# LayerNorm shift rows added by accumulating DMAs, gMLP's v normalised on ScalarE, and gates summed along the free dimension

## The chip, the cores and the metric

The kernel runs on one core of one Trainium2 chip. The metric is device time in microseconds (us), the median of several runs. A profile is one execution of the same program. In its rows PE is TensorE's matmuls, PEld its weight loads, DVE VectorE, ACT ScalarE, POOL GpSimd, and SP SyncE, which here issues DMA.

## The reference, cut to what matters

Two layers (l = 0, 1) with three sub-layers each work on x of 256 rows by 1024 columns. Each sub-layer scales and shifts its input by numbers computed from a vector c, runs a block, multiplies the block's output by a gate that is also computed from c, and normalises:

```
c_act = silu(c)
mod   = c_act @ w_ada[l] + b_ada[l]              # nine rows of 1024 for each layer
shift, scl, gate = mod[3i], mod[3i+1], 1 + mod[3i+2]
h = x * (1 + scl[i]) + shift[i]
x = layer_norm(ALPHA * x + w * gate[i] * block(h), ln_g[l, i], ln_b[l, i])
layer_norm(x, g, b) = (x - mean) * rsqrt(var + 1e-5) * g + b
```

Block 0 and block 2 are SwiGLU feed-forwards (w = 0.5, inner width 2816). Block 1 is the gMLP in layer 0 and chunked attention in layer 1 (w = 1). In the gMLP, z = gelu(h @ w_in + b_in) is split into u and v (2048 columns each); v gets a layer_norm of its own with rows v_g and v_b, then for each of 8 groups of 256 columns a 128x128 matrix mixes its rows, and the result is multiplied into u and by w_out.

## The kernel before, in words

The 256 rows are two tiles t = 0, 1 of 128 rows; X[t] is the residual, 128x1024 in SBUF. Weights stream through once: SP loads a tile `raw` of 128x1024 fp32 (512 KB, six buffers), ACT casts it to `hi` (L215), DVE makes the rest `lo` = raw - hi (L216), and PE does three matmuls of 128x512 for each half of the tile: hi with the high part of the activations (L259), lo with the high part (L260), hi with the low part (L262).

The 20 rows of modulation are computed in between ("steps", one 512 KB tile of w_ada each, pumped between weight units). Fourteen of them (those in the list COLS) are columns: a tile has the 128 features on the partitions and the 1024 elements of c along the free dimension, and DVE multiplies by a row of c and sums along the free dimension in one instruction (L125), which is followed by a read of its accumulator; the result is a tile `mod` of 128x8. The other six are the gates (l, 2), (l, 5), (l, 8), which are needed as rows, repeated on all partitions: DVE adds c[p] * raw into a 128x1024 accumulator `acc` (L154, eight tiles for each gate; POOL clears it, L150, and the bias row is loaded into it, L151). Five ticks of the work list later (LAG_M) `finish_gate` splits acc into ghi (ACT, L166) and glo (DVE, L167), and PE sums over the partitions by matmuls with a matrix of ones (L172, L173, four for each gate); ACT writes the row `gate` from PSUM (L174). `add_y` (L350) multiplies a block's output by it.

After a sub-layer `normalise` computes mean and variance on DVE; POOL takes the power -0.5 (L368), for the gMLP's v as for X; DVE normalises X (L374). `residual_affine` then multiplies X by the row lng (L393) and adds the row lnb (L394), in halves of 512 columns, some 20 ticks later. The rows are loaded, repeated on all partitions, by `load_lnrow`; only at the last of the six LayerNorms is the affine part done elsewhere.

In the gMLP, `v_norm` (one call for each t, four tiles V of 128x512) does (v - mu) * v_g (L581) and * rs + v_b (L582) on DVE, out of rows v_g and v_b that SP has loaded.

`after(n, f)` puts f off by n ticks of the work list; each engine then works its own queue in order.

Of the kernel before, what the change touches and what calls it, by code (L numbers as in the profile page):

```python
# [8 lines left out]
F32 = mybir.dt.float32  # L9
F32R = mybir.dt.float32r  # L10
AF = mybir.ActivationFunctionType
ALU = mybir.AluOpType
AX = mybir.AxisListType

P = 128
D = 1024
SEQ = 256
NT = SEQ // P
KD = D // P
# [19 lines left out]
LAG_A = 4  # L39
LAG_H = (4, 4)  # L40
LAG_H2 = 2
LAG_M = 5

LAG_R = (20, 16)

# [1 line left out]

COLS = [(0, 1), (0, 0), (0, 4), (0, 3), (0, 7), (0, 6), (1, 1), (1, 0), ("kv", 1), ("kv", 0),
        (1, 4), (1, 3), (1, 7), (1, 6)]


@with_exitstack
def encoder_kernel(ctx, tc, a, out):
    nc = tc.nc
    PSUM = bass.MemoryType.PSUM
    pool = lambda name, bufs, **kw: ctx.enter_context(tc.tile_pool(name=name, bufs=bufs, **kw))

    const = pool("const", 1)
    rawp = pool("rawp", N_RAW)
    unitp = pool("unitp", N_UNIT)  # L60
    htp = pool("htp", 8)
    bigp = pool("bigp", N_BIG)
    xp = pool("xp", 1)
    rowp = pool("rowp", 1)
    accp = pool("accp", 1)
    sgp = pool("sgp", 5)
    ap_ = pool("ap", 4)
    bcp = pool("bcp", 2)
    smp = pool("smp", 4)
    modp = pool("modp", 6)  # L70
    ps = pool("ps", 6, space=PSUM)
    pt = pool("pt", 2, space=PSUM)
# [3 lines left out]
    def nm(s):  # L76
        uid[0] += 1
        return f"{s}_{uid[0]}"
# [5 lines left out]
    X = [xp.tile([P, D], F32, name=f"X{t}") for t in range(NT)]  # L84
    c_act = const.tile([P, KD], F32, name="c_act")
    bcol = const.tile([P, len(COLS), KD], F32, name="bcol")
    ident = const.tile([P, P], F32, name="ident")
    make_identity(nc, ident)
    nc.scalar.activation(c_act, c_raw, AF.Silu)
    ones = const.tile([P, P], F32, name="ones")  # L90
    nc.vector.memset(ones, 1.0)
    ones_r = const.tile([P, P], F32R, name="ones_r")
    nc.vector.tensor_copy(ones_r, ones)
    mhalf = const.tile([P, 1], F32, name="mhalf")
    nc.vector.memset(mhalf, -0.5)
    wcol = {}
    for w in (0.5, 1.0):
        wcol[w] = const.tile([P, 1], F32, name=f"wcol{int(2 * w)}")
        nc.vector.memset(wcol[w], w)
    lncols = const.tile([P, 2, 6, KD], F32, name="lncols")  # L100
    bs_sb = const.tile([P, NG], F32, name="bs_sb")
    wsT = const.tile([P, NG, P], F32, name="wsT")
# [1 line left out]
    def load_first():  # L104

        nc.sync.dma_start(out=bcol, in_=a["b_cols"])
        nc.vector.tensor_scalar(bcol[:, 0::2], bcol[:, 0::2], 1.0, None, op0=ALU.add)

    def load_small():
        for t in range(NT):  # L110
# [18 lines left out]
    def col_slice(key):  # L129
        ci = COLS.index(key)  # L130
        st = {}

        def step(j):
            if j == 0:
                st["m"] = modp.tile([P, KD], F32, tag="mod", name=nm("mod"))
            column(ci, j, st["m"])
            if j == KD - 1:
                mods[key] = st["m"]
        return [lambda j=j: step(j) for j in range(KD)]

    def gate_slice(key):
        w_src = a["w_gate"][key[0] * 3 + key[1] // 3].rearrange("(p j) n -> p j n", j=KD)
        b_src = a["b_gate"][key[0] * 3 + key[1] // 3][None, :]
        finish = finish_gate(key, 1.0 if key[1] == 5 else 0.5)
        st = {}

        def step(j):
            if j == 0:
                st["acc"] = accp.tile([P, D], F32, tag="acc", name=nm("acc"))
                nc.gpsimd.memset(st["acc"], 0.0)  # L150
                nc.sync.dma_start(out=st["acc"][0:1, :], in_=b_src)  # L151
            raw = rawp.tile([P, D], F32, tag="raw", name=nm("raw"))
            nc.sync.dma_start(out=raw, in_=w_src[:, j, :])
            nc.vector.scalar_tensor_tensor(st["acc"], raw, c_act[:, j:j + 1], st["acc"],  # L154
                                           op0=ALU.mult, op1=ALU.add)
            if j == KD - 1:
                after(LAG_M, lambda: finish(st["acc"]))
        return [lambda j=j: step(j) for j in range(KD)]

    mods = {}  # L160

    def finish_gate(key, w):
        def f(acc):
            hi = unitp.tile([P, D], F32R, tag="hi", name=nm("ghi"))
            lo = unitp.tile([P, D], F32R, tag="lo", name=nm("glo"))
            nc.scalar.copy(hi, acc)  # L166
            nc.vector.tensor_tensor(lo, acc, hi.bitcast(F32), op=ALU.subtract)  # L167
            g = rowp.tile([P, D], F32, tag="gate", name=nm("gate"))
            for n in range(2):
                sl = slice(n * 512, (n + 1) * 512)  # L170
                tp = pt.tile([P, 512], F32, tag="pt", name=nm("gps"))
                nc.tensor.matmul(tp, lhsT=ones_r, rhs=hi[:, sl], start=True, stop=False)  # L172
                nc.tensor.matmul(tp, lhsT=ones_r, rhs=lo[:, sl], start=False, stop=True)  # L173
                nc.scalar.activation(g[:, sl], tp, AF.Identity, bias=wcol[w], scale=w)  # L174
            mods[key] = g
        return f

    def mk_slice(key):
        return col_slice(key) if key in COLS else gate_slice(key)

    ada = {"steps": [], "credit": 0.0}

    def ada_phase(*parts):

        for _, s in ada["steps"]:
            s()
        ada["steps"] = [(units / (KD * len(keys)), s) for keys, units in parts
                        for k in keys for s in mk_slice(k)]
        ada["credit"] = 0.0

    def pump():
# [9 lines left out]
    def small_dma(out_, in_):  # L201

        with tc.issue_after(last["dma"].ins):
            nc.sync.dma_start(out=out_, in_=in_)
# [62 lines left out]
    def after(n, fn):  # L267
        late.append([n, fn])
# [91 lines left out]
    def rstd_of(parts):  # L360
        stats = smp.tile([P, len(parts), 6], F32, tag=f"st{len(parts)}", name=nm("st"))
        for i, x_ in enumerate(parts):
            nc.vector.bn_stats(out=stats[:, i, :], in_=x_)  # L363
        mv = smp.tile([P, 2], F32, tag="mv", name=nm("mv"))
        nc.vector.bn_aggr(out=mv, in_=stats)
        rs = smp.tile([P, 2], F32, tag="rs", name=nm("rs"))
        nc.vector.tensor_scalar(rs[:, 0:1], mv[:, 1:2], EPS, None, op0=ALU.add)
        nc.gpsimd.tensor_tensor(rs[:, 1:2], rs[:, 0:1], mhalf, op=ALU.pow)  # L368
        return mv[:, 0:1], rs[:, 1:2]
# [6 lines left out]
    lnrow = {}  # L376

    def load_lnrow(ln):
        g = rowp.tile([P, D], F32, tag="lng", name=nm("lng"))
        b = rowp.tile([P, D], F32, tag="lnb", name=nm("lnb"))  # L380
        small_dma(g, a["ln_g"][ln:ln + 1, :].partition_broadcast(P))
        small_dma(b, a["ln_b"][ln:ln + 1, :].partition_broadcast(P))
        lnrow[ln] = (g, b)

    waiting = [[], []]

    def residual_affine(t, ln):

        g, b = lnrow[ln]

        def part(sl):
            with tc.issue_after(last["lo"].ins):
                nc.vector.tensor_tensor(X[t][:, sl], X[t][:, sl], g[:, sl], op=ALU.mult)  # L393
                nc.vector.tensor_tensor(X[t][:, sl], X[t][:, sl], b[:, sl], op=ALU.add)  # L394
            waiting[t].remove(sl)
        waiting[t] = [slice(i * 512, (i + 1) * 512) for i in range(2)]
        for i in range(2):
            after(LAG_R[t] + 2 * i, lambda sl=waiting[t][i]: part(sl))
# [163 lines left out]
    def gmlp(gate, done, before_last):  # L562
# [11 lines left out]
        vrow = []  # L574

        def v_norm(t):
            mu, rs = rstd_of(V[t])
            for n in range(4):
                v = V[t][n]
                g, b = vrow[n]  # L580
                nc.vector.scalar_tensor_tensor(v, v, mu, g, op0=ALU.subtract, op1=ALU.mult)  # L581
                nc.vector.scalar_tensor_tensor(v, v, rs, b, op0=ALU.mult, op1=ALU.add)  # L582

        for vi in range(2):
            c0 = GH + vi * D
            units = row_units(w_in, 0, KD, c0)
            bts = bias_tiles(c0)
            if vi == 1:
                for n in range(4):
                    sl = slice(n * 512, (n + 1) * 512)  # L590
                    gb = []
                    for src in ("v_g", "v_b"):
                        x_ = bigp.tile([P, 512], F32, tag="b", name=nm(src))
                        small_dma(x_, a[src][:, sl].partition_broadcast(P))
                        gb.append(x_)
                    vrow.append(gb)
            for t in range(NT):
                accs = gemm_pass(Later(hT, t), units, KD)
                for n in range(2):
                    v = V[t][vi * 2 + n]  # L600
                    nc.vector.tensor_tensor(v, accs[n], bts[n], op=ALU.add)
                    nc.scalar.activation(v, v, AF.Gelu)
                if vi == 1:
                    v_norm(t)
# [186 lines left out]
    def step(ln):  # L791
# [5 lines left out]
        start=lambda: (ada_phase(([(0, 2)], 13), ([(0, 4), (0, 3)], 24)),))  # L797
# [68 lines left out]
```

## Time and profile before

| | us |
|---|---|
| median of 3 runs | 1056.77 (1054.62 to 1057.21) |
| the profiled execution's own time | 1057.11 |
| span of the profiled execution | 1055.3 |
| PE busy | 1028.1 (97%) |
| PEld busy | 842.2 (80%) |
| DVE busy | 856.0 (81%) |
| ACT busy | 519.9 (49%) |
| POOL busy | 24.5 (2%) |
| data queue of the DMA engines | 76.6% of 16 engines' span, 267 GB/s |

The span is what the profile's rows cover; the execution's own time is 1.8 us more. Busy shares are means over the whole span. In a row of the timeline the first number is the start and the second how long the instructions lasted, from the first's start to the last's end; back-to-back instructions overlap, so what one costs its engine is read from start to start.

### The profile page before, as it was taken

The numbers are of one execution on the slowest core, as the hardware profiler recorded it, in microseconds if no ns is written. First come the engines' busy times: TensorE is split into PE (matmuls) and PEld (weight loads), VectorE is DVE, ScalarE is ACT, GpSimd is POOL, SyncE is SP. The second block draws the span as 40 slices with busy tenths as digits, with TensorE's granted clock in tenths as the row PEclk, the third lists the DMA queues.
The fourth block names the chain that finished last, engine by engine and source line by source line (L and its number), as shares of the span: only waits on it lengthen the run. The fifth ranks groups of instructions, "written<-read, shape, count | busy, mean of one in ns | idle before, by whom it ended". The sixth has DMA issues, their size and how long they took to land. (4 is left out here: it accounts for less than half of the span.)

```text
span 1055.3 us, 13549 instructions
## 1 busy us (share of the span) xinstructions
PE 1028.1 (97%) x4804; PEld 842.2 (80%) x4804; DVE 856.0 (81%) x1185; ACT 519.9 (49%) x729; POOL 24.5 (2%) x39
## 2 busy tenths in 40 slices
PE   7999999999999999999999999999999999999997
PEld 6768888887778788888877888887787788888886
DVE  6888897799999899998679986858998969555535
ACT  4455455454436464444547444453658557345520
POOL 0000000001000100000000000000000000000000
PEclk9999999999999999999999999999999999999999
DMA  9989898687799779999847897757799837645621
GB/s 332 375 315 354 282 348 340 209 280 258 264 333 324 252 251 337 361 344 338 294 152 238 310 344 263 262 203 275 244 353 307 291 101 256 224 160 189 235 76 40
DMA packets 110160, 282.58 MB, mean 268 GB/s; under 512 B 9734, under 2 KB 22278, under 8 KB 110092
## 3 DMA queue, kind: packets, MB, share of 16 engines
q1 hardware_dynamic: 110092, 281.72, 76.6%
q8 instruction: 37, 0.61, 0.2%
q14 instruction: 31, 0.25, 0.1%
HBM read 280.63 MB, written 1.05 MB: 267 GB/s over the span
## 5 line engine op out<-in xcount | busy, mean ns | idle before, releaser
L215 ACT CAST hi<-raw 128x1024 fp32r<-128x1024 f32 x328 | 341.4, 1057 | 228.5 <-DMA raw<-ffn_gu 73.4
L216 DVE TENSOR_TENSOR lo<-raw,hi 128x1024 fp32r<-128x1024 f32 x328 | 394.3, 1220 | 54.8 <-ACT hi L215 49.4
L259 PE MATMUL acc<-hi,hh 128*128 128x512 f32 x928 | 362.1, 396 | 5.1 <-ACT hh L498 3.6
L260 PE MATMUL acc<-lo,hh 128*128 128x512 f32 x928 | 358.5, 392 | 3.5 <-DVE lo L216 2.9
L262 PE MATMUL acc<-hi,hl 128*128 128x512 f32 x928 | 292.9, 391 | 0.1
L259 PEld LDWEIGHTS acc<-hi,hh 128*128 128x128 f32 x928 | 174.4, 188 | 44.0 <-ACT hh L498 5.5
L260 PEld LDWEIGHTS acc<-lo,hh 128*128 128x128 f32 x928 | 174.3, 188 | 40.4 <-DVE lo L216 4.9
L262 PEld LDWEIGHTS acc<-hi,hl 128*128 128x128 f32 x928 | 174.3, 188 | 37.5 <-DVE hl L295 0.8
L259 PE MATMUL acc<-hi,th 128*128 128x512 f32 (+1 forms) x432 | 164.2, 387 | 0.4 <-ACT th L294 0.4
L260 PE MATMUL acc<-lo,th 128*128 128x512 f32 (+1 forms) x432 | 162.2, 383 | 0.1
L125 DVE CUSTOM_DVE_ANT_0 raw<-raw,c_row,bcol 128x1024 f32<-128x1024 f32 x112 | 143.2, 1279 | 19.9 <-DMA raw<-w_cols 19.9
L262 PE MATMUL acc<-hi,tl 128*128 128x512 f32 (+1 forms) x432 | 143.3, 383 | 0.0
L259 PEld LDWEIGHTS acc<-hi,th 128*128 128x128 f32 x432 | 81.1, 188 | 16.0 <-ACT th L294 0.9
L260 PEld LDWEIGHTS acc<-lo,th 128*128 128x128 f32 x432 | 80.9, 188 | 16.2 <-DVE lo L216 1.4
L262 PEld LDWEIGHTS acc<-hi,tl 128*128 128x128 f32 x432 | 80.6, 188 | 15.9
L313 ACT ACTIVATE hf<-hp,B,A 128x128 f32<-128x128 f32 x96 | 36.6, 476 | 66.2 <-PE hp L325 66.2
L154 DVE SCALAR_TENSOR_TENSOR acc<-raw,c_act,acc 128x1024 f32<-128x1024 f32 x48 | 61.4, 1278 | 6.1 <-DMA raw<-w_gate 6.1
L419 ACT ACTIVATE sg<-acc 128x512 f32<-128x512 f32 (+1 forms) x48 | 27.0, 563 | 79.2 <-PE acc L262 78.7
L295 DVE TENSOR_TENSOR tl<-tp,th 128x512 fp32r<-128x512 f32 (+1 forms) x56 | 36.3, 650 | 36.2 <-ACT th L294 36.1
L420 DVE TENSOR_TENSOR a<-acc,sg 128x512 f32<-128x512 f32 (+1 forms) x48 | 30.9, 643 | 40.5 <-ACT sg L419 40.4
L294 ACT CAST th<-tp 128x512 fp32r<-128x512 f32 (+1 forms) x56 | 30.9, 553 | 63.9 <-PE tp L301 63.7
L350 DVE TENSOR_TENSOR gy<-acc,gate 128x512 f32<-128x512 f32 (+1 forms) x49 | 32.0, 675 | 20.6 <-PE acc L262 20.5
(101 smaller groups left out, 582.3 us busy)
## 6 DMA issues: line engine op xcount, KB each, us to landing
raw<-ffn_gu SPq DMA_DIRECT2D x160, 512.0 KB, 5.8
raw<-w_cols SPq DMA_DIRECT2D x112, 512.0 KB, 5.5
raw<-ffn_down SPq DMA_DIRECT2D x88, 512.0 KB, 5.3
raw<-w_gate SPq DMA_DIRECT2D x48, 512.0 KB, 5.0
raw<-w_in SPq DMA_DIRECT2D x32, 512.0 KB, 5.3
raw<-ffn_gu SPq DMA_DIRECT2D x32, 256.0 KB, 4.5
raw<-w_out SPq DMA_DIRECT2D x16, 512.0 KB, 5.7
raw<-w_kv SPq DMA_DIRECT2D x16, 512.0 KB, 5.4
```

The costliest lines, as they stand in the source:

```text
L125: nc.vector.tensor_tensor_reduce(out=raw, in0=raw, in1=c_row, scale=1.0, scalar=bcol[:, ci, j:j + 1], op0=ALU.mult, op1=ALU.add, accum_out ...
L154: nc.vector.scalar_tensor_tensor(st["acc"], raw, c_act[:, j:j + 1], st["acc"], op0=ALU.mult, op1=ALU.add)
L215: nc.scalar.copy(hi, raw)
L216: last["lo"] = eng.tensor_tensor(lo, raw, hi.bitcast(F32), op=ALU.subtract)
L259: nc.tensor.matmul(acc, lhsT=xh, rhs=wh[:, sl], start=k == 0, stop=False)
L260: nc.tensor.matmul(acc, lhsT=xh, rhs=wl[:, sl], start=False, stop=False)
L262: nc.tensor.matmul(acc, lhsT=xl, rhs=wh[:, sl], start=False, stop=k == nk - 1)
L294: nc.scalar.copy(hi, src_ps)
L295: nc.vector.tensor_tensor(lo, src_ps, hi.bitcast(F32), op=ALU.subtract)
L313: nc.scalar.activation(hf[:, sl], tp[:, sl], AF.Identity, bias=B[:, j:j + 1], scale=A[:, j:j + 1])
L350: nc.vector.tensor_tensor(tmp, acc[:, :c1 - c0], g[:, sl], op=ALU.mult)
L420: nc.vector.tensor_tensor(av[:, :wd], u, sg[:, :wd], op=ALU.mult)
```

## The change

Three things change.

1. The gates become columns too: they are appended to COLS, their weights lie in w_cols, and L122 of the changed kernel (L125 before) sums them. `finish_gate` multiplies the 128x8 result by 0.5 where w is 0.5 (DVE, L146), and POOL's queue writes it to a row `grow` in DRAM (L148) two ticks later; three ticks after that SP loads the row, repeated on all partitions, as `gate` (L179). The accumulator, its clearing, its split, the ones matrix and the matmuls go.
2. In `residual_affine` DVE multiplies X by lng (L369), and an accumulating DMA issued by POOL adds ln_b from DRAM into X (L370), 256 KB each, 20 in all. The row lnb is loaded only for the last LayerNorm.
3. In `v_norm` DVE computes off = -mu * rs (L556), ACT does v * rs + off (L559), DVE multiplies by v_g (L560), and an accumulating DMA issued by POOL adds v_b from DRAM (L561), 256 KB each, 8 in all. The row v_b is not loaded.

```diff
-LAG_M = 5
+LAG_M = 2
+LAG_G = 3
+N_MODS = len(COLS)
+COLS += [(l, m) for l in range(2) for m in (2, 5, 8)]
...
-def finish_gate(key, w):
-        def f(acc):
-            hi = unitp.tile([P, D], F32R, tag="hi", name=nm("ghi"))
-            lo = unitp.tile([P, D], F32R, tag="lo", name=nm("glo"))
-            nc.scalar.copy(hi, acc)
-            nc.vector.tensor_tensor(lo, acc, hi.bitcast(F32), op=ALU.subtract)
-            g = rowp.tile([P, D], F32, tag="gate", name=nm("gate"))
-            for n in range(2):
-                ...
-                nc.tensor.matmul(tp, lhsT=ones_r, rhs=hi[:, sl], start=True, stop=False)
-                nc.tensor.matmul(tp, lhsT=ones_r, rhs=lo[:, sl], start=False, stop=True)
-                nc.scalar.activation(g[:, sl], tp, AF.Identity, bias=wcol[w], scale=w)
-            mods[key] = g
+    def finish_gate(key, m):
+        if key[1] != 5:
+            nc.vector.tensor_scalar(m, m, 0.5, None, op0=ALU.mult)
+        row = dramp.tile([1, D], F32, tag="grow", name=nm("grow"))
+        nc.gpsimd.dma_start(out=row.rearrange("o (p j) -> (o p) j", j=KD), in_=m)
+
+        def load():
+            g = gatep.tile([P, D], F32, tag="gate", name=nm("gate"))
+            small_dma(g, row.partition_broadcast(P))
+            mods[key] = g
+        after(LAG_G, load)
...
             with tc.issue_after(last["lo"].ins):
                 nc.vector.tensor_tensor(X[t][:, sl], X[t][:, sl], g[:, sl], op=ALU.mult)
-                nc.vector.tensor_tensor(X[t][:, sl], X[t][:, sl], b[:, sl], op=ALU.add)
+            nc.gpsimd.dma_start(out=X[t][:, sl], in_=a["ln_b"][ln:ln + 1, sl].partition_broadcast(P),
+                                accum_op=ALU.add)
...
         def v_norm(t):
             mu, rs = rstd_of(V[t])
+            off = smp.tile([P, 1], F32, tag="off", name=nm("off"))
+            nc.vector.scalar_tensor_tensor(off, mu, -1.0, rs, op0=ALU.mult, op1=ALU.mult)
             for n in range(4):
                 v = V[t][n]
-                g, b = vrow[n]
-                nc.vector.scalar_tensor_tensor(v, v, mu, g, op0=ALU.subtract, op1=ALU.mult)
-                nc.vector.scalar_tensor_tensor(v, v, rs, b, op0=ALU.mult, op1=ALU.add)
+                nc.scalar.activation(v, v, AF.Identity, bias=off, scale=rs)
+                nc.vector.tensor_tensor(v, v, vrow[n], op=ALU.mult)
+                nc.gpsimd.dma_start(
+                    out=v, in_=a["v_b"][:, n * 512:(n + 1) * 512].partition_broadcast(P),
+                    accum_op=ALU.add)
```

On DVE this is the place of v_norm for t = 0, in the kernel before: V_1823 to V_1826 are the four tiles of v, mv and rs their mean and power, lo a weight unit's rest.

```order
L365 BN_AGGR mv_2181<-st_2176 128x2 [waits DVE_49]
L216 TENSOR_TENSOR lo_2288<-raw_2285,hi_2287 128x1024 [waits DMAHW7_49]
L367 TENSOR_SCALAR rs_2183<-mv_2181 128x1 [waits DVE_49]
L581 SCALAR_TENSOR_TENSOR V_1823<-V_1823,mv_2181,v_g_2038 128x512 [waits DMAHW3_49]
L581 SCALAR_TENSOR_TENSOR V_1824<-V_1824,mv_2181,v_g_2042 128x512 [waits DMAHW5_49]
L582 SCALAR_TENSOR_TENSOR V_1823<-V_1823,rs_2183,v_b_2040 128x512 [waits DMAHW4_49,DVE_49,Pool_49]
```

The same place in the changed kernel, where V_1806 to V_1809 are the tiles of v:

```order
L340 BN_AGGR mv_2154<-st_2149 128x2 [waits DVE_49]
L122 ISA raw_2295,mod_2279<-raw_2295,c_row,bcol 128x1024 [waits DMAHW0_49]
L122 ISA mod_2279 128x1
L342 TENSOR_SCALAR rs_2156<-mv_2154 128x1 [waits DVE_49]
L556 SCALAR_TENSOR_TENSOR off_2159<-mv_2154,rs_2156 128x1 [waits Pool_49]
L191 TENSOR_TENSOR lo_2307<-raw_2304,hi_2306 128x1024 [waits DMAHW1_49,Activation_49]
L560 TENSOR_TENSOR V_1806<-V_1806,v_g_2019 128x512 [waits Activation_49]
L560 TENSOR_TENSOR V_1807<-V_1807,v_g_2021 128x512 [waits DMAHW2_49,Activation_49]
```

Before, the first instruction behind rs that waits for POOL is the third of the V instructions; in the changed kernel it is the one right behind rs, and the four multiplications of V wait for ACT.

On POOL this is the same stretch of the changed kernel; X_105 and X_106 are the two residual tiles, and grow_2181 is the row of the gate (0, 5).

```order
L370 DMA X_106<-ln_b 128x512 [waits DMAHW3_49,DVE_49,PE_49]
L148 DMA grow_2181<-mod_1838 128x8 [waits DVE_49]
L370 DMA X_106<-ln_b 128x512 [waits DVE_49,PE_49]
L343 TENSOR_TENSOR rs_2156<-rs_2156,mhalf 128x1 [waits DVE_49]
L561 DMA V_1806<-v_b 128x512 [waits DVE_49]
L561 DMA V_1807<-v_b 128x512 [waits DVE_49]
L561 DMA V_1808<-v_b 128x512 [waits DMASW0_49,DVE_49]
L561 DMA V_1809<-v_b 128x512 [waits DMASW1_49,DVE_49]
L343 TENSOR_TENSOR rs_2238<-rs_2238,mhalf 128x1 [waits DVE_49]
```

Before, the two powers (L368) followed each other with nothing between them; now the DMA issues of X, of the gate's row and of V stand in the same queue.

On SP this is where the first gate's row is loaded in the changed kernel: raw_899 holds the last tile of the gate's weights, grow_921 its row in DRAM.

```order
L121 DMA raw_899<-w_cols 128x1024 [waits DMAHW1_49,DVE_49]
L184 DMA raw_908<-ffn_down 128x1024 [waits DMAHW0_49,DVE_49]
L184 DMA raw_923<-ffn_down 128x1024 [waits DMAHW3_49,DVE_49]
L121 DMA raw_930<-w_cols 128x1024 [waits DMAHW4_49,DMAHW2_49,DVE_49]
L184 DMA raw_939<-ffn_down 128x1024 [waits DVE_49]
L121 DMA raw_945<-w_cols 128x1024 [waits DMAHW6_49,DVE_49]
L184 DMA raw_954<-ffn_down 128x1024 [waits DMAHW5_49,DVE_49]
L179 DMA gate_966<-grow_921 128x1024 [waits DMASW0_49]
L184 DMA raw_968<-ffn_down 128x1024 [waits DMAHW7_49,DMAHW0_49,DVE_49]
```

The load of the gate's row is new in SP's queue; six weight loads stand between the gate's last tile and it, and weight loads stand behind it.

## Rows read from the trace of the kernel before

**Rows 1.** Busy time by stretch: span, then busy us per engine (instructions), clock, DMA, GB/s.

```profile
220.00:262.00 42.00, 42.00 (x187) 34.88 (x186) 42.00 (x60) 19.18 (x23) 2.92 (x3) 1.00 0.83 283
262.00:325.00 63.00, 59.84 (x265) 46.89 (x265) 58.91 (x85) 25.59 (x30) 0.00 (x0) 1.00 0.86 301
325.00:1025.00 700.00, 692.57 (x3279) 569.02 (x3278) 559.35 (x784) 366.16 (x534) 14.54 (x23) 1.00 0.75 258
sum 1056.00, PE 1028.11 PEld 842.19 DVE 855.98 ACT 519.91 POOL 24.53; mean PE 171.35 PEld 140.37 DVE 142.66 ACT 86.65 POOL 4.09
```

**Rows 2.** What PE waited for from 262 to 325: total us, times, longest.

```profile
PE acc L260 <- DVE lo L216: 1.7, 1, 1.7
PE acc L259 <- ACT hi L215: 0.9, 2, 0.6
```

**Rows 3.** PE's timeline around a gate's four matmuls.

```profile
392.79 0.39 PE L172 MATMUL gps<-ghi,ones_r 128*128 128x512 f32 x1
...
393.70 0.39 PE L259 MATMUL acc<-hi,hh 128*128 128x512 f32 x1
```

**Rows 4.** DVE's timeline in v_norm's stretch.

```profile
239.26 1.22 DVE L167 TENSOR_TENSOR glo<-acc,ghi 128x1024 fp32r<-128x1024 f32 x1
240.39 1.29 DVE L601 TENSOR_TENSOR V<-acc,bin 128x512 f32<-128x512 f32 x2
...
245.27 1.41 DVE L581 SCALAR_TENSOR_TENSOR V<-V,mv,v_g 128x512 f32<-128x512 f32 x2
...
250.57 1.22 DVE L216 TENSOR_TENSOR lo<-raw,hi 128x1024 fp32r<-128x1024 f32 x1
251.70 1.28 DVE L601 TENSOR_TENSOR V<-acc,bin 128x512 f32<-128x512 f32 x2
252.90 1.28 DVE L125 CUSTOM_DVE_ANT_0 raw<-raw,c_row,bcol 128x1024 f32<-128x1024 f32 x1
```

**Rows 5.** Groups by line: busy us, mean ns of one, idle before them and its releaser.

```profile
L125 DVE CUSTOM_DVE_ANT_0 raw<-raw,c_row,bcol 128x1024 f32<-128x1024 f32 x112 | 143.2, 1279 | 19.9 <-DMA raw<-w_cols 19.9
L154 DVE SCALAR_TENSOR_TENSOR acc<-raw,c_act,acc 128x1024 f32<-128x1024 f32 x48 | 61.4, 1278 | 6.1 <-DMA raw<-w_gate 6.1
L125 DVE DVE_READ_ACCUMULATOR2_ANT mod<- 128x1 f32 x112 | 9.3, 83 | 0.0
L174 ACT ACTIVATE gate<-gps,wcol 128x512 f32<-128x512 f32 x12 | 7.6, 680 | 8.3 <-PE gps L173 8.3
```

**Rows 6.** POOL's timeline in v_norm's stretch.

```profile
240.54 0.95 POOL L150 MEMSET acc<- 128x1024 f32 x1 [26.94 <-DVE glo L167]
245.44 0.98 POOL L368 TENSOR_TENSOR rs<-rs,mhalf 128x1 f32<-128x1 f32 x1 [3.94 <-DVE rs L367]
```

**Rows 7.** DMA issues by tile: count, KB each, median us from issue to landing.

```profile
lnb<-ln_b SPq DMA_DIRECT2D x6, 512.0 KB, 8.0
...
v_g<-v_g SPq DMA_DIRECT2D x4, 256.0 KB, 7.1
...
out<-X SPq DMA_DIRECT2D x3, 256.0 KB, 2.0
```

**Rows 8.** PE's timeline: the first spatial matmuls, which read V.

```profile
254.88 1.89 PE L614 MATMUL sp<-V,wsT 128*128 128x256 f32 x8
```

**Rows 9.** The gate (0, 2): its last summing instruction, SP's loads behind it, its first use.

```profile
93.92 1.27 DVE L154 SCALAR_TENSOR_TENSOR acc<-raw,c_act,acc 128x1024 f32<-128x1024 f32 x1
95.23 1.47 SPq L209 DMA_DIRECT2D raw<-ffn_down  x2
114.90 1.29 DVE L350 TENSOR_TENSOR gy<-acc,gate 128x512 f32<-128x512 f32 x2 [0.74 <-PE acc L262]
```

**Rows 10.** One X tile: the addition of lnb, and the first use behind it.

```profile
575.62 1.28 DVE L394 TENSOR_TENSOR X<-X,lnb 128x512 f32<-128x512 f32 x2
597.16 1.28 DVE L352 SCALAR_TENSOR_TENSOR X<-X,gy 128x512 f32<-128x512 f32 x2
```

More of the change, by code (lines that the diff above doesn't have):

```diff
@@ L64, in encoder_kernel @@
     rowp = pool("rowp", 1)
-    accp = pool("accp", 1)
+    gatep = pool("gatep", 2)
+    dramp = pool("dramp", 2, space=bass.MemoryType.DRAM)
     sgp = pool("sgp", 5)
@@ L89, in encoder_kernel @@
     nc.scalar.activation(c_act, c_raw, AF.Silu)
[L90 to L93, printed above, removed]
     mhalf = const.tile([P, 1], F32, name="mhalf")
     nc.vector.memset(mhalf, -0.5)
[L96 to L99, printed above, removed]
     lncols = const.tile([P, 2, 6, KD], F32, name="lncols")
@@ L106, in load_first @@
         nc.sync.dma_start(out=bcol, in_=a["b_cols"])
-        nc.vector.tensor_scalar(bcol[:, 0::2], bcol[:, 0::2], 1.0, None, op0=ALU.add)
+        for sl in (slice(0, N_MODS, 2), slice(N_MODS, None)):
+            nc.vector.tensor_scalar(bcol[:, sl], bcol[:, sl], 1.0, None, op0=ALU.add)
     def load_small():
@@ L136, in step @@
             column(ci, j, st["m"])
-            if j == KD - 1:
+            if j < KD - 1:
+                return
+            if ci < N_MODS:
                 mods[key] = st["m"]
[L139 to L157, printed above, removed]
+            else:
+                after(LAG_M, lambda: finish_gate(key, st["m"]))
@@ L158, in gate_slice @@
         return [lambda j=j: step(j) for j in range(KD)]
     mods = {}
-    def finish_gate(key, w):
-        def f(acc):
-            hi = unitp.tile([P, D], F32R, tag="hi", name=nm("ghi"))
-            lo = unitp.tile([P, D], F32R, tag="lo", name=nm("glo"))
-            nc.scalar.copy(hi, acc)
-            nc.vector.tensor_tensor(lo, acc, hi.bitcast(F32), op=ALU.subtract)
-            g = rowp.tile([P, D], F32, tag="gate", name=nm("gate"))
-            for n in range(2):
-                sl = slice(n * 512, (n + 1) * 512)
-                tp = pt.tile([P, 512], F32, tag="pt", name=nm("gps"))
-                nc.tensor.matmul(tp, lhsT=ones_r, rhs=hi[:, sl], start=True, stop=False)
-                nc.tensor.matmul(tp, lhsT=ones_r, rhs=lo[:, sl], start=False, stop=True)
-                nc.scalar.activation(g[:, sl], tp, AF.Identity, bias=wcol[w], scale=w)
+    def finish_gate(key, m):
[6 more added lines that the diff above has]
+            small_dma(g, row.partition_broadcast(P))
@@ L175, in f @@
             mods[key] = g
-        return f
-    def mk_slice(key):
-        return col_slice(key) if key in COLS else gate_slice(key)
+        after(LAG_G, load)
     ada = {"steps": [], "credit": 0.0}
@@ L187, in ada_phase @@
         ada["steps"] = [(units / (KD * len(keys)), s) for keys, units in parts
-                        for k in keys for s in mk_slice(k)]
+                        for k in keys for s in col_slice(k)]
         ada["credit"] = 0.0
@@ L378, in load_lnrow @@
     def load_lnrow(ln):
[L379 to L383, printed above, removed]
+        lnrow[ln] = []
+        for tag, src in (("lng", "ln_g"), ("lnb", "ln_b"))[:2 if ln == 5 else 1]:
+            row = rowp.tile([P, D], F32, tag=tag, name=nm(tag))
+            small_dma(row, a[src][ln:ln + 1, :].partition_broadcast(P))
+            lnrow[ln].append(row)
     waiting = [[], []]
     def residual_affine(t, ln):
-        g, b = lnrow[ln]
+        g, = lnrow[ln]
         def part(sl):
@@ L589, in gmlp @@
                 for n in range(4):
[L590 to L596, printed above, removed]
+                    g = bigp.tile([P, 512], F32, tag="b", name=nm("v_g"))
+                    small_dma(g, a["v_g"][:, n * 512:(n + 1) * 512].partition_broadcast(P))
+                    vrow.append(g)
             for t in range(NT):
@@ L840 @@
     b_of = lambda l, m: (n(b_ada_kv).reshape(-1) if l == "kv" else n(b_ada)[l])[m * D:(m + 1) * D]
-    gates = [(l, m) for l in range(2) for m in (2, 5, 8)]
+    feat = lambda i: np.arange(D) if i < N_MODS else np.arange(D).reshape(P, KD).T.reshape(-1)
     by_p = np.arange(D).reshape(P, KD).T.reshape(-1)
@@ L845 @@
         "xT": n(x)[0].T.reshape(2, KD // 2, P, SEQ).transpose(2, 0, 1, 3).reshape(P, 2, D),
-        "w_cols": np.stack([w_of(*k)[by_p].T for k in COLS]),
-        "b_cols": np.stack([b_of(*k).reshape(KD, P) for k in COLS]).transpose(2, 0, 1),
-        "w_gate": np.stack([w_of(*k) for k in gates]), "b_gate": np.stack([b_of(*k) for k in gates]),
+        "w_cols": np.stack([w_of(*k)[by_p].T[feat(i)] for i, k in enumerate(COLS)]),
+        "b_cols": np.stack([b_of(*k)[feat(i)].reshape(KD, P) for i, k in enumerate(COLS)])
+                  .transpose(2, 0, 1),
         "ln_g": n(ln_g).reshape(6, D), "ln_b": n(ln_b).reshape(6, D),
```

## The prediction

> **What bounds the kernel now.** I first read busy time by stretch: PE is busy 1028.1 of 1055.3 us, so TensorE's queue is the bound over most of the span, and a removed matmul is worth its spacing [rows 1]. Then I looked for stretches where that isn't so. From 220 to 262 PE and DVE are both busy for the full 42.00 us; from 262 to 325 PE is idle for 63.00 - 59.84 = 3.16 us, with DVE busy for 58.91; from 325 to 1025 PE is idle for only 7.4 of 700 [rows 1]. So DVE matters in one place, the gMLP, and there by lateness: it falls behind while it normalises v. The waits of 262 to 325 name it: PE waits 1.7 us once for a lo, and 0.9 for hi, which ACT can cast only when a raw buffer has come free and been filled [rows 2]. Elsewhere what DVE, ACT or POOL save lies beside matmuls and returns nothing.
>
> **The gates.** Six gates had four matmuls each. Around one of them four matmuls take 393.70 - 392.79 = 0.91 us of PE's time, 0.227 each, and PE does not stop before or behind them [rows 3]. They go, and nothing replaces them on PE: 24 x 0.227 = 5.45 us, straight off the bound. That is the surest term.
>
> DVE's summing costs the same in either form, 1278 ns before and 1279 as a column, plus 83 ns for each read of the accumulator [rows 5]; 48 x 0.083 = 4.0 us, spread under matmuls save in the gMLP. glo goes as well (1.13 us of DVE from start to start [rows 4]), as do ghi and the two writes of `gate` on ACT (680 ns each [rows 5]). None of these was waited for outside the gMLP by rows that I saw, so I cost them at nothing there; the cover is PE's own queue.
>
> The new path of a gate has a wait in it. For (0, 2) the last sum ends at 93.92 + 1.27 = 95.2. I add 0.15 for the multiplication by 0.5 (an estimate from the small DVE operations), 1.0 for POOL's issue (its instructions take 0.95 to 0.98 [rows 6]) and 2.0 for the write to land (SBUF to DRAM, 256 KB, 2.0 [rows 7]): 98.3. SP reaches the load of the gate's row behind the sixth weight load after the gate's last tile. There are six raw buffers, so that sixth load takes the gate's last buffer, and goes out at 95.2 [rows 9]. SP then stands until 98.3, 2.7 us, and the weight loads behind it go out up to 1.9 us late. The row itself, by the 8.0 us of an equal load [rows 7], lands at about 106, ahead of its use at 114.90 [rows 9], so add_y doesn't wait. What the lateness of the loads costs PE lies between 0 and 1.9 us for each gate, 0 to 11.4 together. PE hardly waits for weights except in the gMLP [rows 1, 2], where one gate, (0, 5), is finished; I take 0.8 us, somewhat under half of one block, and nothing for the others.
>
> **The residual.** 20 additions on DVE go, 0.60 us each from start to start (two 128x512 operations in 251.70 to 252.90 [rows 4]). Outside the gMLP they lie beside PE and are worth nothing; four of them are in the gMLP stretch. The accumulating transfers that take their place appear in no row. For one of 256 KB the lower bound is its share of the rate, 0.262 MB / 283 GB/s = 0.93 us of the DMA engines [rows 1], the upper, from issue to landing, the 7.1 to 8.0 us of a broadcast row [rows 7]. Both ends are hidden: X is next read 597.16 - 576.90 = 20.3 us after the addition [rows 10].
>
> **v_norm.** In the gMLP stretch DVE loses 16 V instructions, (250.57 - 245.27) x 2 = 10.6 us, four lnb additions, 2.4, and glo, 1.1: 14.1. It gains 8 multiplications at 0.60, 4.8; two off at 0.15, 0.3; four accumulator reads, 0.3; and one wait. The power on POOL runs from 245.44 to 246.42, and was covered by the two L581 that began at 245.27 [rows 4, 6]; off now stands right behind rs, so DVE waits from 245.3 to 246.5, 1.2 us, with a lo queued behind it (for t = 1 another lo stands ahead of off, which covers most of it). Together 6.6; DVE is 7.5 us ahead. If the multiplications are paced by ACT instead (680 ns for the nearest ACT row [rows 5]), it is 8 x 0.08 = 0.6 less. ACT is busy 19.18 of 42 us and has room for 8 x 0.68 = 5.4.
>
> These 7.5 us are not worth 7.5. PE was never idle from 220 to 262; what the lateness cost are the 3.16 us afterwards [rows 1], so that is the cap, and 0 the other end. The larger wait, 1.7 us for a lo, is far less than 7.5, so I take the whole 3.16.
>
> V itself comes out of an accumulating transfer now. In the old timing the multiplications for t = 0 would be done at about 250.5. PE wanted V at 254.88 [rows 8]; in the changed program 30 more weight matmuls stand ahead of the first spatial one, 6.8 us, less the 0.91 of a gate's: 260.8. That leaves 10 us, against 7.1 to 8.0 for a load [rows 7]: hidden, with little to spare.
>
> All of it is 1057.1 - 5.45 - 3.16 + 0.8 = 1049.3 for the profiled execution; it stood 0.34 above the median, so I predict 1049.0 us.
>
> One thing speaks against it: POOL's issues could hold DVE up. The row says that POOL's memset at 240.54 lay beside the V addition at 240.39, which took 1.29 us for two against 1.28 at 251.70 with POOL idle [rows 4, 6]: no lengthening. The Trainium skill, "SBUF — State Buffer", section "Who interferes with whom", says that DVE and GpSimd share a pair of ports, that a DVE operation with two SBUF inputs contends with a GpSimd instruction that reads SBUF, and not with one that only writes. The memset only writes, so this row agrees with the rule but cannot clear the issues, which no row shows.
>
> **The rivals.**
>
> B, only the matmuls come back. In the stretch from 220 to 325 the DMA engines are already busy for 0.83 to 0.86 [rows 1], and hi and lo are late because raw is. Then the new transfers take what DVE gives back: 1057.1 - 5.45 + 0.8 - 0.3 = 1052.1. For it: some PE waits are for hi. Against it: the longest is for lo. Chance 0.13.
>
> D, no change. Thirteen POOL issues fall in the gMLP stretch (12 accumulations and a gate's row). If each keeps DVE for the 0.98 us of a POOL instruction [rows 6], that is 12.7 against the 7.5 gained; DVE, which is full, ends 5.2 later, and so does PE: 1057.1 - 5.45 + 0.8 + 5.2 = 1057.7, less 0.3: 1057.4. From about 9.0 us of such holding on it is within 0.3% of before. Against it stands the unlengthened row. Chance 0.15, with other mishaps of that size, between 1053.6 and 1058.
>
> C, slower: the accumulating transfer is dear for the DMA engines. Net, the stretch gains 12 x 0.262 + 0.52 (the gate's row) - 1.05 (v_b's tiles) = 2.6 MB, 9.3 us at 283 GB/s, against idle DMA time of 0.17 x 42 + 0.14 x 63 = 15.9 us [rows 1]: it fits. If an accumulation moves at a third of that rate, 2.8 us, then 12 x 1.85 = 22.2 us are added, 15.6 don't fit, weights come late by that, and the time is 1057.1 - 5.45 + 0.8 + 15.6 - 0.3 = 1067.8. It ends slower by over 0.3% from 2.1 us for each 256 KB on (12 x 1.2 = 14.4 = 6.6 to spare + 7.8). For it: nothing in the trace shows the price. Against it: plain transfers reach 301 GB/s here. Chance 0.11. The Trainium skill, "Collectives: The Full Stack", section "The bandwidth ceiling: the fold count and why AG ≠ RS ≠ AR", says that an add in the DMA engines reads two sources and so ran at about half the rate of a copy; by that, an estimate, an accumulation takes 1.9 us, just short of C's point, and the time would be about 1056.7. No run here shows it yet.
>
> The forecast itself, A, has 0.61, with a range of its own from 1045.5 to 1051.
>
> **How the numbers follow.** A change under 0.3%, 3.2 us, can hardly be told from none; faster is below 1053.6, slower above 1059.9. A and nearly all of B are faster: 0.72. D and a little of B are the same: 0.16. C, with a little of D: 0.12. The low end, 1045.5, is A with the gate wait at nothing and 2.7 us more of the 7.4 that PE idles from 325 to 1025 [rows 1]. The high end, 1056.5, takes in B and most of D; D's rest and C, under 2 in 10, stay out.
>
> **What would show it.** Right: PE has 24 matmuls fewer; from 262 to 325 PE idles under 1 us; the V additions keep 0.60 us beside POOL's issues; DVE waits once, about 1.2 us, behind rs. Wrong: spatial matmuls waiting for a DMA into V; DVE operations longer while POOL issues; raw loads landing much later than now between 228 and 262, or SP standing several us for a gate's row with PE short of lo behind it.

## The result, and the profile after

The changed kernel takes 1069.88 us (median of 4 runs, 1067.64 to 1071.9) against 1056.42 of the kernel before on the same chip: 1.012 times, 95% interval 1.0095 to 1.0145. It is slower by about 13 us, where 7.8 us faster was forecast and the range ended at 1056.5; the time lies near rival C's, 1067.8. The ratios, here and below, are worked out from all runs of the two kernels, not from the medians beside them. The profiled execution took 1069.97, its span is 1068.2.

Busy time by stretch in the changed kernel, columns as in [rows 1]; its last stretch but one is 10 us longer:

```profile
220.00:262.00 42.00, 38.62 (x167) 31.03 (x166) 36.02 (x52) 20.54 (x25) 7.38 (x9) 0.99 0.98 308
262.00:325.00 63.00, 58.09 (x248) 46.63 (x248) 55.15 (x82) 27.14 (x32) 5.91 (x6) 0.95 0.94 322
325.00:1035.00 710.00, 694.83 (x3277) 571.11 (x3276) 547.56 (x802) 358.27 (x523) 27.12 (x40) 1.00 0.76 261
...
sum 1068.00, PE 1028.03 PEld 842.37 DVE 834.35 ACT 513.65 POOL 46.39; mean PE 171.34 PEld 140.40 DVE 139.06 ACT 85.61 POOL 7.73
```

Against [rows 1], PE's idle time from 220 to 262 went from 0 to 3.4 us, from 262 to 325 from 3.2 to 4.9, and behind it from 7.4 to 15.2. DVE is busy 21.6 us less over the whole kernel, and it didn't help: in the gMLP (220 to 325) DVE now waits, and the DMA engines are busy for 0.94 to 0.98 instead of 0.83 to 0.86. PE's busy time is the same to 0.1 us though 24 matmuls are gone. That is the clock: in three places PE is granted a lower clock behind a stall. PE alone, stretches of 5 us (span, busy, clock, DMA, GB/s):

```profile
255.00:260.00 5.00, 1.75 (x7) 1.00 1.00 215
260.00:265.00 5.00, 4.62 (x13) 0.66 1.06 278
265.00:270.00 5.00, 2.61 (x12) 1.00 1.06 361
...
770.00:775.00 5.00, 1.21 (x6) 0.82 1.06 356
775.00:780.00 5.00, 5.00 (x17) 0.50 1.03 348
780.00:785.00 5.00, 5.00 (x24) 1.00 0.97 332
```

At 0.50, which is 1.2 GHz, matmuls of 128x512 begin 0.43 us apart, and at 1.00, 2.4 GHz, 0.23 (PE's timeline):

```profile
777.01 0.63 PE L234 MATMUL acc<-hi,hh 128*128 128x512 f32 x1
777.44 0.63 PE L235 MATMUL acc<-lo,hh 128*128 128x512 f32 x1
...
780.00 0.39 PE L235 MATMUL acc<-lo,hh 128*128 128x512 f32 x1
780.23 0.39 PE L234 MATMUL acc<-hi,hh 128*128 128x512 f32 x1
```

Summed over all such stretches up to 1045 us, 5 us x (1 - clock) is 6.8 us, and 1.75 in the kernel before, there all in the first 20 us. This counts idle moments of these stretches too, so it is an estimate; PE's unchanged busy time says the same, since the 5.45 us of the matmuls went and as much came back. Between the two spans (12.9 us) PE's idle time grew by 13.0, from 1055.3 - 1028.1 = 27.2 to 1068.2 - 1028.0 = 40.2; the low clock adds 5.05 and the matmuls take 5.45 away, 12.6 in all.

What PE waits for in the changed kernel (total, times, longest):

```profile
PE acc L235 <- DVE lo L191: 7.9, 6, 2.7
PE tp L276 <- DVE a L397: 5.1, 4, 2.2
PE tp L626 <- ACT k L623: 4.1, 2, 3.8
PE acc L234 <- ACT hi L190: 3.0, 2, 2.4
```

The second and third rows look like waits for other work than weights. The timeline of one shows that they aren't:

```profile
578.19 0.88 POOL L370 DMA_DIRECT2D X<-ln_b  x1 [2.25 <-PE acc L237]
578.77 0.88 POOL L148 DMA_DIRECT2D grow<-mod  x1
579.42 1.13 POOL L370 DMA_DIRECT2D X<-ln_b  x1
...
581.46 0.33 SPq L121 DMA_DIRECT2D raw<-w_cols  x1
585.49 0.33 SPq L179 DMA_DIRECT2D gate<-grow  x1
585.92 0.37 SPq L184 DMA_DIRECT2D raw<-ffn_down  x1
...
592.68 1.05 ACT L190 CAST hi<-raw 128x1024 fp32r<-128x1024 f32 x1 [5.90 <-DMA raw<-ffn_down]
...
595.18 0.39 ACT L396 ACTIVATE sg<-acc 128x256 f32<-128x256 f32 x1
...
596.52 0.41 DVE L397 TENSOR_TENSOR a<-acc,sg 128x256 f32<-128x256 f32 x1
...
597.08 0.41 PE L276 MATMUL tp<-ident,a 128*128 128x128 f32 x2 [2.22 <-DVE a L397]
```

POOL issues accumulations and the gate's row; SP stands until the row has been written (585.49) and issues a weight load late; ACT waits 5.90 us for it with a hi, and sg stands behind that hi in ACT's queue; then come a on DVE and PE. The waits that end at 268.75, 298.15 and 774.39 (2.4, 1.95 and 3.8 us) go back to a raw tile that lands late as well. The one at 260.12, 2.7 us, does so in part: ACT had waited 5.58 us for a raw tile, and then its four normalisations of v stood ahead of the next hi for 2.94 us.

Two causes offer themselves, and each forecasts where the loss goes. **S**: SP's standing at the gate's row. **A** (T in the first expectations): the 28 accumulating transfers, which crowd the weight loads. In the changed kernel both show (SP's waits, and the issues of POOL by size and time to landing):

```profile
SPq L179 <- DMA grow<-mod: 19.8, 6, 5.0
```

```profile
X<-ln_b POOLq DMA_DIRECT2D x20, 256.0 KB, 7.7
...
V<-v_b POOLq DMA_DIRECT2D x8, 256.0 KB, 7.7
...
grow<-mod POOLq DMA_DIRECT2D x6, 4.0 KB, 4.8
```

### The profile page after: what moved, and what is told of

Read it like the earlier page. It is cut to its first block, busy times and chain, and to the rows that moved or that the text cites. A ratio compares the mean times of both kernels' runs of the same rounds, so it can differ in the third digit from the quotient of the medians.

```text
span 1068.2 us, 13588 instructions
## 1 busy us (share of the span) xinstructions
PE 1028.0 (96%) x4780; PEld 842.4 (79%) x4780; DVE 834.4 (78%) x1202; ACT 513.7 (48%) x719; POOL 46.4 (4%) x67
## 5 line engine op out<-in xcount | busy, mean ns | idle before, releaser
L122 DVE CUSTOM_DVE_ANT_0 raw<-raw,c_row,bcol 128x1024 f32<-128x1024 f32 x160 | 204.5, 1278 | 30.3 <-DMA raw<-w_cols 29.7
L343 POOL TENSOR_TENSOR rs<-rs,mhalf 128x1 f32<-128x1 f32 x14 | 13.9, 995 | 682.1 <-DVE rs L342 682.1
```

The costliest lines, as they stand in the source:

```text
L122: nc.vector.tensor_tensor_reduce(out=raw, in0=raw, in1=c_row, scale=1.0, scalar=bcol[:, ci, j:j + 1], op0=ALU.mult, op1=ALU.add, accum_out ...
```

## The experiments

All ratios are to the kernel before on the same chip, with 95% intervals; 0.1% is 1.06 us. Readings of a trace are of one execution.

**One part at a time, and SP's wait taken away.** Three kernels are the kernel before with one of the three hunks of the diff: the gates, `residual_affine` with `load_lnrow`, or `v_norm` with its row loads. The fourth is the changed kernel with one line different:

```diff
-            small_dma(g, row.partition_broadcast(P))
+            nc.gpsimd.dma_start(out=g, in_=row.partition_broadcast(P))
```

The gates alone: 

> Only the gates are changed (columns, a row through DRAM, SP loads it); residual and v_norm as before. Theory S (SP stands at each gate's row until POOL's small write has landed, 19.8 us in all in the changed kernel, and the weight loads behind it come late): most of the loss is here, 1062 to 1070 us, SP waits for the row 15 us or more. Theory T (the accumulating transfers crowd the weight loads and the row's write): without them the write lands in 2 to 3 us, SP waits under 10 us in all, and the time is 1051 to 1055, the 24 matmuls less.

The residual alone: 

> Only the residual is changed (20 additions on DVE become accumulating DMAs of POOL). Theory S: nothing of the loss is here, 1055 to 1058. Theory T: slower, 1060 or more, with PE short of hi and lo behind the accumulations.

v_norm alone: 

> Only v_norm is changed (ACT normalises, DVE multiplies by v_g, POOL's accumulating DMA adds v_b). Theory S: PE's stall in the gMLP goes, 1053 to 1056. Theory T: 1058 or more, with raw loads landing late between 225 and 325 us. A third, N, that the spatial matmuls wait for V out of the DMA: a wait of PE for a DMA into V.

The gate's row loaded by POOL: 

> All three changes, but the gate's row is loaded by POOL's queue, not SP's: the same bytes and the same instructions on PE and DVE, and no wait of SP for the row's write. Theory S: the loss goes, 1048 to 1054. Theory T: it stays for the larger part, 1062 or more.

| kernel | median us | ratio | interval |
|---|---|---|---|
| gates alone | 1055.03 | 0.9982 | 0.9962 to 1.0002 |
| residual alone | 1071.98 | 1.0137 | 1.0106 to 1.0169 |
| v_norm alone | 1061.39 | 1.0035 | 1.0013 to 1.0058 |
| all, row by POOL | 1071.82 | 1.0128 | 1.0093 to 1.0164 |

S falls: with SP's wait gone the loss is all there, and the residual alone, which has no such wait, makes all of it. SP stands even longer in the gates alone:

```profile
SPq L179 <- DMA grow<-mod: 24.4, 6, 5.5
```

and that kernel is not slower. That it stands there for 24.4 us is against what A expected, under 10; the write landed after 3.7 us there, and after 4.8 with the accumulations. The third theory for v_norm, N, has some ground: the first spatial matmul there waited 1.2 us, though the profile names no releaser for it. The longest stall of that kernel in this stretch, 4.0 us, and one of 1.1 are matmuls that wait for a product with u, and u stands on ACT behind a hi that waits for its raw tile.

**What an accumulation costs.** Three variants of the residual alone, one with plain copies, one without transfers, one with the multiplications and accumulations six ticks later; and the gates alone with POOL loading the row:

```diff
-            nc.gpsimd.dma_start(out=X[t][:, sl], in_=a["ln_b"][ln:ln + 1, sl].partition_broadcast(P),
-                                accum_op=ALU.add)
+            nc.gpsimd.dma_start(out=X[t][:, sl], in_=a["ln_b"][ln:ln + 1, sl].partition_broadcast(P))
```

```diff
-LAG_R = (20, 16)
+LAG_R = (26, 22)
```

In the first two ln_b isn't added. Plain copies: 

> The residual change alone, with plain copies in place of the 20 accumulations: same queue, places, waits and bytes (X is overwritten by ln_b, so this part is left out of the computation). Theory A (an accumulation holds the DMA engines about twice as long as a copy, 1.49 us against some 0.8 by the queue's shares, and weight loads behind it come late): half the loss or more goes, 1058 to 1065. Theory Q (any transfer on a second queue at that time does it): no change, 1069 to 1073.

No transfer: 

> The residual change alone, with the 20 accumulations left out (ln_b isn't added). If the transfers are the cause (A or Q): no loss, 1053 to 1057. If the loss comes from the other rearrangement, such as DVE's order, it stays at 1065 or more.

Six ticks later: 

> The residual change alone, with the multiplications and so the accumulations six ticks later. If the loss hangs on what loads they meet, the time moves by several us either way, 1060 to 1076; if it is a fixed price of each accumulation, it stays at 1069 to 1073.

The gates alone, row by POOL: 

> The gates alone (1055.0 against 1057.6 of before, SP standing 24.4 us in all for the rows), with the row loaded by POOL's queue. If SP's standing is what keeps that version from the 5.45 us of its matmuls: 1050 to 1053. If it costs nothing: 1054 to 1056.

| kernel | median us | ratio | interval |
|---|---|---|---|
| plain copies | 1065.59 | 1.0078 | 1.0051 to 1.0105 |
| no transfer | 1059.06 | 1.0014 | 0.9991 to 1.0037 |
| later | 1074.07 | 1.0157 | 1.0117 to 1.0197 |
| gates alone, row by POOL | 1052.92 | 0.9956 | 0.9932 to 0.998 |

Without transfers the loss is gone within the interval, though the median is 2 us above the range that was expected: the loss is theirs. About half of it remains with plain copies. Issuing later is not told apart from issuing as before. The gates come out faster once SP doesn't stand: 0.44%, 4.7 us.

The queue's rows (packets, MB, share of 16 engines over the span) say how long these transfers' packets took, and so how long they held the DMA engines. Residual alone, with accumulations, and with copies:

```profile
q0 software_dynamic: 2880, 5.24, 2.8%
```

```profile
q0 software_dynamic: 1600, 5.24, 1.8%
```

0.028 x 1066.0 / 20 = 1.49 us for each accumulation, and 0.018 x 1063.8 / 20 = 0.96 for each copy. The copy comes to the 0.93 that the prediction took as the lower bound. Weight loads around them pay. In the stretch from 565 to 600 the loads (count, KB, median us to landing) with accumulations and without transfers:

```profile
raw<-ffn_down SPq DMA_DIRECT2D x6, 512.0 KB, 6.8
...
X<-ln_b POOLq DMA_DIRECT2D x4, 256.0 KB, 7.5
```

```profile
raw<-ffn_down SPq DMA_DIRECT2D x4, 512.0 KB, 4.7
```

That is one tile's loads in one stretch. Over the 20 to 27 us from each of the five groups of transfers on, the medians of all 512 KB weight loads, averaged by count, come to 6.8 us with accumulations, 7.0 with copies and 5.7 without transfers. So loads beside either kind are late by about a microsecond, and the lateness alone doesn't say why accumulations cost about twice as much.

**By packets, by source, and v_norm without accumulations.** Whole rows in one accumulation, the row lnb in SBUF as the source, and the v_norm of the change with v_b loaded as a row and added by DVE, alone and with the gates (row by POOL):

```diff
-            nc.gpsimd.dma_start(out=X[t][:, sl], in_=a["ln_b"][ln:ln + 1, sl].partition_broadcast(P),
-                                accum_op=ALU.add)
+            if not waiting[t]:
+                nc.gpsimd.dma_start(out=X[t], in_=a["ln_b"][ln:ln + 1, :].partition_broadcast(P),
+                                    accum_op=ALU.add)
```

```diff
-                nc.vector.tensor_tensor(X[t][:, sl], X[t][:, sl], b[:, sl], op=ALU.add)
+            nc.gpsimd.dma_start(out=X[t][:, sl], in_=b[:, sl], accum_op=ALU.add)
```

```diff
                 nc.scalar.activation(v, v, AF.Identity, bias=off, scale=rs)
                 nc.vector.tensor_tensor(v, v, g, op=ALU.mult)
+                nc.vector.tensor_tensor(v, v, b, op=ALU.add)
```

v_norm with DVE's addition: 

> v_norm alone, ACT normalising as in the changed kernel, but v_b loaded as a row and added by DVE, without accumulations. The eight accumulations hold the DMA engines for 8 x 1.46 = 11.7 us by their queue's share; if they are what costs v_norm its 0.35% (theory A), this is 1055 to 1058. If it is ACT, where the normalisation and the wait for POOL stand ahead of hi casts, it stays at 1059 to 1062.

The gates and that v_norm: 

> The gates with the row loaded by POOL, and the v_norm of e9; residual as before: no accumulation anywhere. Theory A: about the time of the gates alone with POOL's row, 1051 to 1055, faster than before. If ACT's normalisation costs: 1055 or more.

Whole rows: 

> The residual alone, with one accumulation of 128x1024 for each tile instead of two of 128x512: the same bytes in rows of 4 KB instead of 2 KB. If an accumulation costs by packets, the queue's share falls from 1.49 us to about 1.0 for each 256 KB, and the time to 1061 to 1067. If it costs by bytes, share and time stay, 1068 to 1073.

The row in SBUF: 

> The residual alone, with the row lnb loaded into SBUF as before and accumulated from there, so that no accumulation reads DRAM. If the read of DRAM is what makes an accumulation dear: share near 0.8 us for each 256 KB and 1060 to 1066. If the add itself (two reads and a write) is: share about 1.5 us and 1069 to 1076, since the row's loads stay as well.

| kernel | median us | ratio | interval |
|---|---|---|---|
| v_norm, DVE adds | 1059.28 | 1.0028 | 1.0013 to 1.0042 |
| gates, and that v_norm | 1052.37 | 0.9962 | 0.9945 to 0.9979 |
| whole rows | 1073.92 | 1.0158 | 1.0132 to 1.0183 |
| row in SBUF | 1065.27 | 1.0083 | 1.0063 to 1.0104 |

The queue's rows of the whole rows and of the row in SBUF:

```profile
q0 software_dynamic: 1440, 5.24, 2.8%
```

```profile
q0 software_dynamic: 2880, 5.24, 2.7%
```

Packets are not the price: half as many (1440) took the same 2.8%, and no time was saved. The row in SBUF took 2.7%, 1.43 us each, and lost 0.5% less than the row in DRAM, so the engines' share is not the whole price either. And v_norm's loss is there without its accumulations: against expectation, they are not shown to cost anything in that kernel, while the rest of it (ACT's normalisation, and off behind rs) costs 0.28%. Beside the gates the same costs nothing that shows (0.9962 against 0.9956).

**Source against add, and the whole change without accumulations.** The row in SBUF with a plain copy; accumulations of 128 different rows of x in DRAM; and all three changes, row by POOL, with the 28 accumulations left out:

```diff
-            nc.gpsimd.dma_start(out=X[t][:, sl], in_=b[:, sl], accum_op=ALU.add)
+            nc.gpsimd.dma_start(out=X[t][:, sl], in_=b[:, sl])
```

```diff
-            nc.gpsimd.dma_start(out=X[t][:, sl], in_=a["ln_b"][ln:ln + 1, sl].partition_broadcast(P),
+            nc.gpsimd.dma_start(out=X[t][:, sl], in_=a["x"][t * P:(t + 1) * P, sl],
                                 accum_op=ALU.add)
```

Copy out of SBUF: 

> As the run with the row in SBUF, but plain copies in place of accumulations (X is overwritten by the row, so this part is left out). If the add is what is left of the price there: 1056 to 1060, under 0.4% above before. If any transfer into X at that place costs the same: 1063 to 1067.

Different rows: 

> The residual alone, accumulating 128 different rows of a DRAM array (the input x) instead of 128 times the same 2 KB of ln_b, which is left out. If the many reads of one DRAM row are what is dear: 1063 to 1067, as with the row in SBUF. If any DRAM source is: 1069 to 1073.

All without accumulations: 

> All three changes with the gate's row loaded by POOL, and without the 28 accumulations (ln_b and v_b are left out). If the accumulations are what the changed kernel loses by: 1049 to 1054, the 24 matmuls less, and no low clock behind 225 us. If the rest costs too: 1056 or more.

| kernel | median us | ratio | interval |
|---|---|---|---|
| copy out of SBUF | 1056.45 | 1.0005 | 0.9993 to 1.0017 |
| different rows | 1067.91 | 1.011 | 1.0086 to 1.0134 |
| all, no accumulations | 1051.66 | 0.995 | 0.993 to 0.9969 |

The copy out of SBUF, with its queue's row,

```profile
q0 software_dynamic: 1600, 5.24, 1.3%
```

0.69 us each, costs nothing that shows. It has the same 20 issues on POOL at the same places, so issuing a transfer there is not what costs; and its weight loads, averaged as above, land after 5.9 us, against 6.7 with accumulations out of SBUF. So the four kinds stand in a square: copy from SBUF 0.05%, copy from DRAM 0.78, accumulation from SBUF 0.83, accumulation from DRAM 1.37. The add and the read of DRAM each cost 0.5 to 0.8%, and the intervals of neighbours in the square don't overlap (the two with SBUF also load the row lnb, as before the change). Whether reading one row 128 times is dearer than different rows is not told apart (1.0137 and 1.011, the intervals overlap). And the whole change without accumulations is 0.5% faster than before: the accumulations cost it 1.0128 - 0.995 = 0.018, 19 us, 0.67 for each of 28 on the average. The low clock, which the expectation excluded behind 225 us, came there too: behind a wait of 2.9 us PE was granted 0.70 and 0.61 from 800 to 810.

## Why the prediction was wrong

- **The residual: "Both ends are hidden".** This is the step that failed. It asked when X is read next, 20 us later [rows 10], and that was right: nothing waited for X. It didn't ask what else the DMA engines had to do in those 20 us. An accumulation held them for 1.49 us, weight loads beside it landed later (6.8 against 5.7 us), and the weights are the kernel's supply. The measured price is 1.0137 - 1.0014 = 1.2%, 13 us, for 20 accumulations, where 0 stood. That the transfers cost this is shown by leaving them out; that they do so by way of late weight tiles is read off the traces and wasn't tested by itself.
- **Rival C** had the mechanism, but laid it in the gMLP alone, though over half of PE's added idle time came behind it, where the DMA engines idle for a quarter of the time [rows 1]; and it let it decide only from 2.1 us for each. At 1.49 us it decided all the same. The reason offered is that the idle time of a stretch can't be spent at will: a load goes out when a raw buffer comes free (SP's loads of L184 wait 274.3 us in all for a lo in the changed kernel). That six buffers are too few to bridge several accumulations is inferred from the late loads; more of them weren't tried. The rule of the Trainium skill, "Collectives: The Full Stack", section "The bandwidth ceiling: the fold count and why AG ≠ RS ≠ AR", is about collectives: an add reads two sources and so runs at about half a copy's rate. The runs here agree for the row in SBUF (1.43 against 0.69 us); from DRAM it was 1.49 against 0.96.
- **v_norm, "so I take the whole 3.16".** It failed too. v_norm alone came out 0.35% slower, 3.7 us, and 0.28% slower without its accumulations. The nearest to what the prediction had in mind is the whole change without accumulations (columns as in [rows 1]):

```profile
220.00:262.00 42.00, 40.31 (x177) 32.77 (x175) 39.64 (x60) 21.71 (x27) 4.12 (x4) 1.00 0.91 328
262.00:325.00 63.00, 62.73 (x289) 52.30 (x290) 61.43 (x87) 34.74 (x41) 0.00 (x0) 1.00 0.87 318
```

  Behind 262 PE idles 0.27 us there, under the 1 us that the prediction gave as a sign of being right; but 1.69 us of new idle time stand ahead of it, and the time, 0.995, is not told from the gates' alone, 0.9956. So what DVE gave back made no time that shows. In the residual without transfers, with four additions less on DVE and nothing in their place, PE idled 105 - 101.22 = 3.8 us from 220 to 325, against 3.16 before:

```profile
220.00:325.00 105.00, 101.22 (x446) 81.15 (x445) 97.98 (x137) 44.29 (x53) 2.93 (x3) 1.00 0.82 291
```

  In that kernel ACT waits for raw tiles where DVE had been full (its timeline):

```profile
247.69 1.05 ACT L215 CAST hi<-raw 128x1024 fp32r<-128x1024 f32 x1 [4.81 <-DMA raw<-w_in]
...
262.48 1.06 ACT L215 CAST hi<-raw 128x1024 fp32r<-128x1024 f32 x1 [5.25 <-DMA raw<-w_in]
```

  By these rows DVE was full and the loads were late as well; freeing one left the other. This was rival B's reason, and B's term for this stretch, nothing, was the nearer one.
- **The gates, 5.45 us**, agree: 4.7 us came back with POOL loading the row (2.1 to 7.2 by the interval).
- **SP's wait** was mis-sized. The small write landed after 4.8 us (3.7 in the gates alone), not 2.0; SP stood for 3.3 us at each gate (4.1 in the gates alone), not 2.7. Its price, 0.9982 - 0.9956 = 0.0026, is 2.7 us by the ratios, against 0.8, though the intervals overlap.
- **DVE's wait behind rs** was 0.7 and 0.5 us, not 1.2, since POOL's power took 0.56 the first time and a lo covered most of it the second.
- **Rival D** falls: DVE did not slow beside POOL's issues. In the changed kernel four multiplications by v_g lie beside three of them,

```profile
269.87 2.49 DVE L560 TENSOR_TENSOR V<-V,v_g 128x512 f32<-128x512 f32 x4
270.97 2.69 POOL L561 DMA_DIRECT2D V<-v_b  x3 [5.64 <-DVE V L560]
272.28 1.28 DVE L611 TENSOR_TENSOR u<-acc,bin 128x512 f32<-128x512 f32 x2
```

  and keep (272.28 - 269.87) / 4 = 0.60 us; those of X take 686 ns, and 685 before. The rule of the Trainium skill on the shared ports ("SBUF — State Buffer", section "Who interferes with whom"), that a DVE operation with two SBUF inputs contends with a GpSimd instruction that reads SBUF, cost nothing beside these issues.
- **The low clock** was in no term: about 5 us of the loss in the profiled execution.

Two things stay open: why ACT's normalisation costs 0.28% alone and nothing that shows beside the gates, and why an accumulation out of SBUF costs less time than one out of DRAM while its queue's share is the same.

## What to carry to other kernels

A transfer that nobody waits for is not free in a kernel that lives on streamed weights: ask which loads it lands beside, and how many buffers stand between a late load and the matmul. Moving additions from an engine to the DMA engines cost time here although these idled for a quarter of most of the span; a mean share of idle time doesn't say that a transfer fits. And a wait of an in-order queue (SP for a small write, ACT's hi for its raw tile) shows up as somebody else's wait; follow it back in time to the first late transfer.

## What was not expected of the hardware

- In the changed kernel PE's waits of 2.7, 1.95 and 3.8 us, behind 250 us, were each followed by stretches of 5 us with a mean granted clock of 0.66, 0.79 and 0.50; others of 2.4, 2.2 and 1.9 us were not. So stalls were paid for about 1.4 times in that execution (5 us on 13).
- An accumulation of 256 KB into SBUF held the 16 DMA engines for 1.43 to 1.49 us, a copy for 0.69 (from SBUF) to 0.96 (from DRAM).
- A 4 KB write from SBUF to DRAM out of POOL's queue took 3.7 to 4.8 us to land, longer than 256 KB out of SP's, 2.0 [rows 7].
